# Seven half-width products in place of eight for most FFN column pairs, and a new map of SBUF

## The chip, the core and the metric

The kernel is one program on one core of a Trainium2 chip. The metric is the device time of one execution in microseconds. TensorE (PE) multiplies, VectorE (DVE) and ScalarE (ACT) work on the operands and results, GpSimd (POOL) does a few subtractions at the start and in the mixers, and SyncE (SP) issues the DMAs.

## The reference

Two layers over 512 rows, 256 context tokens and 256 latent tokens, of width 1024. Each layer is a SwiGLU FFN (inner width 2816), a token mixer and a second FFN. Shift, scale and gate of each sub-layer come from `m = silu(c) @ w_ada + b_ada`, nine modulations of 1024 a layer. Cut to what matters:

```
def swiglu(h, w1, w3, w2):
    return (jax.nn.silu(h @ w1) * (h @ w3)) @ w2
...
for l in range(DEPTH):
    x = x + 0.5 * m[:, 2] * swiglu(modulate(rms_norm(x, norm_g[l, 0]), m[:, 0], m[:, 1]), w1[l, 0], w3[l, 0], w2[l, 0])
    ...
    y, yc = token_mixer(h, hc, w_in[l], ...)
    x = x + m[:, 5] * y
    x = x + 0.5 * m[:, 8] * swiglu(modulate(rms_norm(x, norm_g[l, 2]), m[:, 6], m[:, 7]), w1[l, 1], w3[l, 1], w2[l, 1])
```

The context rows xc go through the same FFNs and mixer, up to the last layer's mixer. So three FFNs have 512 tokens, FFN(0,0), FFN(0,1) and FFN(1,0), and the last, FFN(1,1), has 256.

## The kernel before

**Products.** Every big product runs as three matmuls in fp32r (`mm3`, L280 to L282). Weights come as 512 KB loads (8 k-tiles of 128 rows make the 1024 inputs; one load is 4 k-tiles by 256 columns) into `wraw` (pool `wr`, 4 buffers, queue of SP). ACT rounds them to `whi` (L285) and DVE forms `wlo = wraw - whi` (L286), both in pool `wh`, 4 buffers, so a cast waits until the products have read the buffer four chunks earlier. The inputs are kept in the same two parts, `hhi` and `hlo`, as [feature, token].

**An FFN** takes the 2816 columns as 11 pairs g of 256 columns of w1 and 256 of w3, in two halves (g = 0 to 5 and 6 to 10). A pair is 2 x 8 k-tiles x 2 column tiles x 3 = 96 matmuls of 512 tokens ("x512"; x256 is the same for 256). ACT then takes silu of p1 (L607), DVE multiplies by p3 (L608), and ACT and DVE split the result into `ghi` and `glo`. After each half `to_residual` multiplies them by w2 in four column groups `cg`; the last one of the second half is woven with the entry into the next stage (`handover`), where the first pair (g = 0) of the next FFN is computed too.

**Modulations.** `ada` makes one modulation: eight loads of w_ada (512 KB each), two DVE operations of 128x1024 for each (L208 the first, L210 the others), then a few matmuls. `tick()` spreads these steps over the pairs and the w2 groups of the three 512-token FFNs.

**Order.** Apart from the start and the handovers, which are written out by hand, a scheduler sets the order of instructions on each engine when the program is built; each engine and the SP queue then run in that order, and waits between engines are semaphores. A semaphore wait for a tile in PSUM covers the whole two-bank tile.

**SBUF.** From the bottom: constants up to 28 KiB a partition, `xT` to 44, the inputs `hhi` and `hlo` to 76, `wraw` to 92, `whi` and `wlo` to 124, small tiles to 133, and above that the pools of the stages, with `ghi` and `glo`. So the inputs and the weights lie below 128 KiB, and the gated values above. The mixers' inputs are `hhi_m` and `hlo_m` in the same place; their big products are pg and pj (x512 in layer 0, x256 in layer 1).

## Time and profile before

| | us |
|---|---|
| device time, median of 3 runs (2012.78 to 2013.74) | 2013.01 |
| the profiled execution, its own time | 2012.76 |
| its span, first to last instruction | 2011.0 |
| PE busy in the span | 1981.5 (99%) |
| DVE busy | 1330.9 (66%) |
| ACT busy | 836.3 (42%) |

The span lies 1.76 us below the execution's own time. Busy time of matmuls overlaps, since they are pipelined: the mean of one matmul in a group is longer than the step from one start to the next, and what a product costs is read from the steps in the timeline.

### The profile page before, as it was taken

Reading aid. Unit: us, or ns where it says so; the run is one execution under the profiler, and the core shown is the slowest. Engines: PE = TensorE matmul, PEld = TensorE weight load, DVE = VectorE, ACT = ScalarE, POOL = GpSimd, SP = SyncE. Lnnn points to the kernel's source line nnn. Section 1 sums busy time; section 2 is a strip of 40 time slices with the busy share of each in tenths; the row PEclk is TensorE's granted clock in tenths of the full one; section 3 lists DMA queues with packets and bytes.
Section 4 is the critical chain, followed back from the end, with each engine's and each line's share of the span. In section 5 each row is a group of like instructions: output and inputs, shape, how many; then the busy total and the mean of one; then the engine's idle time right before and its main releaser. Section 6 shows DMA issues by size and latency. Waiting matters only on the chain.

```text
span 2011.0 us, 27970 instructions
## 1 busy us (share of the span) xinstructions
PE 1981.5 (99%) x11087; PEld 1685.1 (84%) x11087; DVE 1330.9 (66%) x2038; ACT 836.3 (42%) x1286; POOL 51.7 (3%) x32
## 2 busy tenths in 40 slices
PE   7999999999999999999999999999999998999998
PEld 5887788898777788988788798877888988899998
DVE  6876666476588655765666566664665679877555
ACT  4432222365476534422122243221323758666443
POOL 2000000000001110000000000000000001110000
PEclk8999999999999999999999999999999999999999
DMA  9655555422213324354555425554553224465663
GB/s 298 217 178 173 172 172 173 115 97 83 77 53 97 118 89 123 120 160 146 176 168 157 134 69 189 178 156 125 166 168 105 64 88 143 145 196 162 187 185 115
DMA packets 240507, 288.47 MB, mean 143 GB/s; under 512 B 14368, under 2 KB 222328, under 8 KB 240120
## 3 DMA queue, kind: packets, MB, share of 16 engines
q1 hardware_dynamic: 240376, 286.69, 46.3%
q8 instruction: 87, 1.43, 0.3%
q14 instruction: 44, 0.36, 0.1%
HBM read 283.50 MB, written 3.15 MB: 143 GB/s over the span
## 4 chain that ended last, share of the span: by engine, by line
PE 92%; DVE 3%; ACT 2%; DMA 2%; issue 1%; POOL 0%; SPq 0%; DVEq 0%; ACTq 0%; POOLq 0%
PE p L280 14%; PE p L281 14%; PE p L282 14%; PE py L280 8%; PE py L281 8%; PE py L282 8%; PE pg L282 3%; PE pg L281 3%; PE pg L280 3%; PE pj L281 2%; PE pj L280 2%; PE pj L282 2%; PE pv L809 1%; PE pv L810 1%; PE pv L811 1%; DMA wada<-w_ada 1%
## 5 line engine op out<-in xcount | busy, mean ns | idle before, releaser
L285 ACT CAST whi<-wraw 128x1024 fp32r<-128x1024 f32 (+2 forms) x408 | 406.4, 1000 | 943.6 <-PE p L281 417.0
L286 DVE TENSOR_TENSOR wlo<-wraw,whi 128x1024 fp32r<-128x1024 f32 (+2 forms) x380 | 445.0, 1177 | 348.4 <-ACT whi L285 347.4
L280 PE MATMUL p<-hhi_f,whi 128*128 128x512 f32 (+1 forms) x1440 | 516.1, 359 | 0.4 <-DVE hhi_f L352 0.4
L282 PE MATMUL p<-hhi_f,wlo 128*128 128x512 f32 (+1 forms) x1440 | 513.3, 356 | 1.1 <-POOL wlo L286 0.6
L281 PE MATMUL p<-hlo_f,whi 128*128 128x512 f32 (+1 forms) x1440 | 513.9, 357 | 0.2
L280 PEld LDWEIGHTS p<-hhi_f,whi 128*128 128x128 f32 x1440 | 272.3, 189 | 48.3 <-ACT whi L285 5.9
L282 PEld LDWEIGHTS p<-hhi_f,wlo 128*128 128x128 f32 x1440 | 272.3, 189 | 41.1 <-POOL wlo L286 1.3
L210 DVE SCALAR_TENSOR_TENSOR aacc<-wada,cs,aacc 128x1024 f32<-128x1024 f32 x224 | 277.3, 1279 | 42.6 <-DMA wada<-w_ada 42.3
L281 PEld LDWEIGHTS p<-hlo_f,whi 128*128 128x128 f32 x1440 | 272.3, 189 | 38.8 <-DVE hlo_f L357 1.0
L280 PE MATMUL py<-ghi,whi 128*128 128x512 f32 (+1 forms) x764 | 269.0, 352 | 0.0
L281 PE MATMUL py<-glo,whi 128*128 128x512 f32 (+1 forms) x764 | 267.6, 350 | 0.0
L282 PE MATMUL py<-ghi,wlo 128*128 128x512 f32 (+1 forms) x764 | 267.5, 350 | 0.0
L280 PEld LDWEIGHTS py<-ghi,whi 128*128 128x128 f32 x764 | 143.9, 188 | 26.1 <-issue 4.2
L282 PEld LDWEIGHTS py<-ghi,wlo 128*128 128x128 f32 x764 | 143.9, 188 | 21.3
L281 PEld LDWEIGHTS py<-glo,whi 128*128 128x128 f32 x764 | 143.9, 188 | 21.0
L280 PE MATMUL pg<-hhi_m,whi 128*128 128x512 f32 (+1 forms) x384 | 132.5, 345 | 0.0
L282 PE MATMUL pg<-hhi_m,wlo 128*128 128x512 f32 (+1 forms) x384 | 130.6, 340 | 1.3 <-DVE wlo L286 1.2
L281 PE MATMUL pg<-hlo_m,whi 128*128 128x512 f32 (+1 forms) x384 | 130.3, 339 | 0.0
L286 POOL TENSOR_TENSOR wlo<-wraw,whi 128x768 fp32r<-128x768 f32 (+2 forms) x28 | 51.5, 1842 | 1732.0 <-ACT whi L285 1675.0
L507 DVE SCALAR_TENSOR_TENSOR xT<-py,gmod,xT 128x256 f32<-128x256 f32 x136 | 59.1, 478 | 54.5 <-PE py L282 54.2
L280 PE MATMUL pj<-hhi_m,whi 128*128 128x256 f32 (+1 forms) x288 | 92.9, 323 | 0.0
L281 PE MATMUL pj<-hlo_m,whi 128*128 128x256 f32 (+1 forms) x288 | 92.7, 322 | 0.2
(270 smaller groups left out, 2525.0 us busy)
## 6 DMA issues: line engine op xcount, KB each, us to landing
wraw<-ffn_w SPq DMA_DIRECT2D x256, 512.0 KB, 3.8
wada<-w_ada SPq DMA_DIRECT2D x128, 512.0 KB, 3.8
wraw<-w_in SPq DMA_DIRECT2D x64, 512.0 KB, 3.6
wada<-w_ada SPq DMA_DIRECT2D x32, 256.0 KB, 6.8
wraw<-w_out SPq DMA_DIRECT2D x16, 512.0 KB, 3.4
wraw<-w_in SPq DMA_DIRECT2D x16, 384.0 KB, 3.4
wraw<-w_in SPq DMA_DIRECT2D x20, 256.0 KB, 3.0
wraw<-ffn_w SPq DMA_DIRECT2D x16, 256.0 KB, 2.7
```

Source lines behind the costliest of these rows:

```text
L210: v.scalar_tensor_tensor(acc[:, t], w, cs[:, k, t:t + 1], acc[:, t], op0=ALU.mult, op1=ALU.add)
L280: te.matmul(o, a, xh, start=start, stop=False)
L281: te.matmul(o, a, xl, start=False, stop=False)
L282: te.matmul(o, b, xh, start=False, stop=stop)
L285: s.copy(hi, src)
L286: eng.tensor_tensor(lo, src, hi.bitcast(F32), ALU.subtract)
L507: v.scalar_tensor_tensor(X[0][:, d, c], acc, gate[:, d, t:t + 1], X[0][:, d, c], op0=ALU.mult, op1=ALU.add)
L809: te.matmul(o, hhi[:, kk, ts], hi[:, k], start=(kk == 0), stop=False)
L810: te.matmul(o, hhi[:, kk, ts], lo[:, k], start=False, stop=False)
L811: te.matmul(o, hlo[:, kk, ts], hi[:, k], start=False, stop=(kk == KD - 1))
```

## The change

**Seven products for eight.** For pairs 3 to 10 of the three 512-token FFNs, the two column blocks (w1, w3), the two halves of the 1024 inputs and the two halves of the tokens make a 2 x 2 by 2 x 2 block product. It is computed with seven block products in place of eight (Winograd's form of Strassen): `seven` has seven calls of `part`, each 24 matmuls x256 (4 k-tiles x 2 column tiles x 3). In the code's order they are called P1 to P7 here. P1, P2, P3, P5, P6 and P7 go into one PSUM tile `pab` (b and c are its two halves), P4 into `pc`. A pair is then 168 matmuls x256.

Around them a pair gets four sums of raw weights on DVE (128x1024: L659, L663, L669, L673), seven casts on ACT and seven subtractions on DVE in place of four of each (the weights of the seven products), three copies out of PSUM on ACT (L656, L661, L665), three adds out of PSUM on DVE (L668, L671, L675), and silu and multiply in halves (L678 to L682). The sums of inputs are made once in each FFN by `Forms` (during g = 1 and 2: 8 DVE operations of 128x1024 and four splits).

**Places.** `sm`, `wraw` (now 5 buffers), `whi`/`wlo` and the stage pools with `ghi`/`glo` come first, below 128 KiB; the sums of inputs, `hhi`/`hlo` and `xT` go to the top, above 128 KiB. Two zones there are shared by several short-lived tiles. In FFN(1,1) the gated values lie in those zones.

**Modulations.** The steps of `ada` leave the seven-product pairs: FFN(0,0) makes modulations 2 to 5 of layer 0 (before 2 to 7), mixer 0 gets 6, 7 and 8, FFN(0,1) makes 0 to 3 of layer 1, FFN(1,0) 4 to 7, FFN(1,1) gets 8. In the 512-token FFNs the ticks come at g = 2 and in `to_residual`.

```diff
     const = ctx.enter_context(tc.tile_pool(name="const", bufs=1))
-    xp = ctx.enter_context(tc.tile_pool(name="xp", bufs=1))
-    hp = ctx.enter_context(tc.tile_pool(name="hp", bufs=1))
-    wr = ctx.enter_context(tc.tile_pool(name="wr", bufs=4))
+    sm = ctx.enter_context(tc.tile_pool(name="sm", bufs=2))
+    wr = ctx.enter_context(tc.tile_pool(name="wr", bufs=5))
     wh = ctx.enter_context(tc.tile_pool(name="wh", bufs=4))
-    sm = ctx.enter_context(tc.tile_pool(name="sm", bufs=2))
+    ctx.enter_context(tc.tile_pool(name="pad", bufs=1)).tile([P, 8], F32, name="pad")
+    xp = ctx.enter_context(tc.tile_pool(name="xp", bufs=1, side="right"))
+    hp = ctx.enter_context(tc.tile_pool(name="hp", bufs=1, side="right"))
+    tz = ctx.enter_context(tc.tile_pool(name="tz", bufs=1, side="right"))
+    sp = ctx.enter_context(tc.tile_pool(name="sp", bufs=1, side="right"))
+    hp.tile([P, 16], F32, name="pad")
     ps = ctx.enter_context(tc.tile_pool(name="ps", bufs=2, space=bass.MemoryType.PSUM))
-    ctx.enter_context(tc.tile_pool(name="shift", bufs=1)).tile([P, 8], F32, name="shift")
+    def zone(i, dt=F32):
+        return tz.tile([P, 3 * D], dt, tag=f"t{i}", name=f"zone{i}")
+    def half_zone(i, dt=F32):
+        return sp.tile([P, 3 * NTOK], dt, tag=f"v{i}", name=f"half{i}")
...
-            ws.append(xi.tile([P, 2, 2, L], F32, tag="wada", name="wada", bufs=16))
+            ws.append(last_wada if q == 3 and k == KD - 2 else
+                      xi.tile([P, 2, 2, L], F32, tag="wada", name="wada", bufs=15))
...
+    class Forms:
+        def __init__(self, norm, fp):
+            hi, lo = norm.hi, norm.lo
+            q = [[(x[:, 4 * c:4 * c + 4, 0:L], x[:, 4 * c:4 * c + 4, L:]) for x in (hi, lo)] for c in range(2)]
+            (h11, h12), (l11, l12) = q[0]
+            (h21, h22), (l21, l22) = q[1]
+            z = [zone(i, F32R).rearrange("p (a k n) -> p a k n", a=3, k=4) for i in range(2)]
+            t = [half_zone(i)[:, 0:D].rearrange("p (k n) -> p k n", k=4) for i in range(2)]
+            t.append(fp.tile([P, 2, D], F32, tag="aacc", name="ft")[:, 0].rearrange("p (k n) -> p k n", k=4))
+            def whole(o, a, b):
+                v.tensor_tensor(o, a.bitcast(F32), b.bitcast(F32), ALU.add)
+            whole(t[0], h11, l11)
+            whole(t[1], h12, l12)
+            whole(t[2], h22, l22)
+            v.tensor_tensor(t[0], t[0], t[1], ALU.subtract)
+            v.tensor_tensor(t[1], t[2], t[1], ALU.subtract)
+            split_act(z[0][:, 0], z[1][:, 0], t[0])
+            split_act(z[0][:, 2], z[1][:, 2], t[1])
+            v.scalar_tensor_tensor(t[0], t[0], -1.0, t[2], op0=ALU.mult, op1=ALU.subtract)
+            whole(t[1], h21, l21)
+            split_act(z[0][:, 1], z[1][:, 1], t[0])
+            v.scalar_tensor_tensor(t[0], t[0], -1.0, t[1], op0=ALU.mult, op1=ALU.subtract)
+            self.fourth = lambda: split_act(h12, l12, t[0])
+            self.b11, self.b21, self.b22, self.t4 = (h11, l11), (h21, l21), (h22, l22), (h12, l12)
+            self.t1, self.t2, self.t3 = ((z[0][:, i], z[1][:, i]) for i in range(3))
+            self.n = 0
+        def places(self):
+            if self.n == 0:
+                self.half = [half_zone(i) for i in range(2)]
+                self.w1 = sp.tile([P, NTOK], F32, tag="w1", name="w1")
+            return [x[:, 2 * NTOK:] for x in self.half] + [self.w1]
+        def sum_place(self):
+            self.n += 1
+            return self.half[self.n % 2][:, 0:D].rearrange("p (k n) -> p k n", k=4)
+    def seven(fm, wa, wb, c0, gt):
+        q1, p5, w1 = fm.places()
+        pab, pc = psum("p1"), psum_bg("p3")
+        b, c, a = pab[:, 0], pab[:, 1], pc[:, 0]
+        def raw(w, i):
+            return load_raw([rowsof(w, 4 * i, 4, c0, 2 * P)], 4, 2 * P)
+        def part(o, w, x, first=False):
+            whi, wlo = split(w, 4, 2 * P)
+            for k in range(4):
+                for m in range(2):
+                    om, cm = o[:, m * L:(m + 1) * L], slice(m * P, (m + 1) * P)
+                    for n, (wt, xt) in enumerate(((whi, x[0]), (whi, x[1]), (wlo, x[0]))):
+                        te.matmul(om, wt[:, k, cm], xt[:, k], start=(first and k == m == n == 0),
+                                  stop=(k == 3 and m == 1 and n == 2), skip_group_check=True)
+        a11 = raw(wa, 0)
+        part(b, a11, fm.b11, True)
+        s.copy(q1, b)
+        a21, a22 = raw(wb, 0), raw(wb, 1)
+        s1 = fm.sum_place()
+        v.tensor_tensor(s1, a21, a22, ALU.add)
+        part(c, s1, fm.t1, True)
+        s.copy(p5, c)
+        s2 = fm.sum_place()
+        v.tensor_tensor(s2, s1, a11, ALU.add)
+        part(b, s2, fm.t2)
+        s.copy(w1, b)
+        a12 = raw(wa, 1)
+        part(a, a12, fm.b21, True)
+        v.tensor_tensor(q1, a, q1, ALU.add)
+        v.tensor_tensor(a21, a21, a11, ALU.add)
+        part(b, a21, fm.t3)
+        v.tensor_tensor(p5, b, p5, ALU.add)
+        s4 = fm.sum_place()
+        v.tensor_tensor(s4, s2, a12, ALU.add)
+        part(c, s4, fm.b22)
+        v.tensor_tensor(w1, c, w1, ALU.add)
+        g1, g2 = gt[:, :, 0:L], gt[:, :, L:]
+        q1, p5, w1, b3 = (x.rearrange("p (m n) -> p m n", m=2) for x in (q1, p5, w1, b))
+        s.activation(g1, q1, AF.Silu)
+        s.activation(g2, w1, AF.Silu)
+        v.scalar_tensor_tensor(g2, p5, -1.0, g2, op0=ALU.mult, op1=ALU.mult)
+        part(b, a22, fm.t4)
+        v.scalar_tensor_tensor(g1, b3, -1.0, g1, op0=ALU.mult, op1=ALU.mult)
...
+        both = nt == NTOK
         with tc.tile_pool(name=f"ffn{l}{f}", bufs=1) as fp:
-            steps = (ada(*m, fp) for m in mods)
-            pending[:] = [x for x in steps]
-            total = len(mods) * (KD + 1)
-            state = [0, 0]
-            def tick():
-                state[0] += 1
-                want = min(total, -(-total * state[0] // 56))
+            pending[:] = [ada(*m, fp) for m in mods]
+            due = [0.0]
+            rates = (1.25, (len(mods) * (KD + 1) - 5) / 20) if both else (0.8, 0.0)
+            def tick(rate):
+                due[0] += rate
+                n = int(due[0] + 1e-6)
+                due[0] -= n
                 with norm.done():
-                    background(want - state[1])
-                state[1] = max(want, state[1])
+                    background(n)
+            def weights(n):
+                if both:
+                    return weight_places(n)
+                return [tuple(fp.tile([P, 4, 2 * P], F32R, name=f"e{i}{x}") for x in ("hi", "lo")) for i in range(n)]
             for half, (g0, g1) in enumerate(((0, 6), (6, 11))):
                 nk = 2 * (g1 - g0)
-                ghi = fp.tile([P, 12, NTOK], F32R, tag="ghi", name="ghi")
-                glo = fp.tile([P, 12, NTOK], F32R, tag="glo", name="glo")
+                if both:
+                    ghi = fp.tile([P, 12, NTOK], F32R, tag="ghi", name="ghi")
+                    glo = fp.tile([P, 12, NTOK], F32R, tag="glo", name="glo")
+                else:
+                    ghi, glo = (zone(i, F32R).rearrange("p (k n) -> p k n", k=12) for i in range(2))
                 for g in range(g0, g1):
+                    j = slice(2 * (g - g0), 2 * (g - g0) + 2)
+                    gt = fp.tile([P, 2, NTOK], F32, tag="gt", name="gt")[:, :, 0:nt]
+                    if both and g > 2:
+                        seven(fm, w1, w3, g * 2 * P, gt)
+                        split_act(ghi[:, j, 0:nt], glo[:, j, 0:nt], gt)
+                        continue
                     p1, p3 = norm.accs if g == 0 else (psum("p1"), psum_bg("p3"))
                     if g > 0:
                         for acc, w in ((p1, w1), (p3, w3)):
                             product(acc, load(w, KD, g * 2 * P), (hhi, hlo), nt)
-                            tick()
-                            tick()
-                    j = slice(2 * (g - g0), 2 * (g - g0) + 2)
-                    gt = fp.tile([P, 2, NTOK], F32, tag="gt", name="gt")[:, :, 0:nt]
+                            if g == 2 or not both:
+                                tick(rates[0])
+                                tick(rates[0])
                     if g == 0 and norm.early:
                         norm.gated(gt)
                     else:
                         s.activation(gt, p1[:, :, 0:nt], AF.Silu)
                         v.tensor_tensor(gt, gt, p3[:, :, 0:nt], ALU.mult)
                     split_act(ghi[:, j, 0:nt], glo[:, j, 0:nt], gt)
-                for _ in to_residual(w2, nk, (ghi, glo), nt, gmod[l][:, f], st if half else None, fp, ("a", "b", "c"), 2 * g0,
+                    if both and g == 1:
+                        with norm.done():
+                            fm = Forms(norm, fp)
+                    if both and g == 2:
+                        fm.fourth()
+                for _ in to_residual(w2, nk, (ghi, glo), nt, gmod[l][:, f], st if half else None, fp, weights, 2 * g0,
                                      then):
-                    tick()
+                    tick(rates[1])
+        assert not pending or next(pending[0], None) is None
...
+            pending[:] = [ada(*m, mp) for m in mods]
+            def tick(n=1):
+                with entry.done():
+                    background(n)
...
                         drain()
+                    tick()
...
-                run(merged(2, psum_bg, mm))
-                mhi = mm.tile([P, KD, NTOK], F32R, name="mhi")
-                mlo = mm.tile([P, KD, NTOK], F32R, name="mlo")
+                for n, _ in enumerate(merged(2, psum_bg, mm)):
+                    tick(n % 4 > 0)
+                mhi = mm.tile([P, KD, nq], F32R, name="mhi")
+                mlo = mm.tile([P, KD, nq], F32R, name="mlo")
                 for d in range(0, KD, 2):
                     split_act(mhi[:, d:d + 2, 0:nq], mlo[:, d:d + 2, 0:nq], mixed[d // 4][:, d % 4:d % 4 + 2])
-                run(to_residual(I["w_out"][l], KD, (mhi, mlo), nq, gmod[l][:, 2], st, mm, ("v", "a"), entry=then))
+                for n, _ in enumerate(to_residual(I["w_out"][l], KD, (mhi, mlo), nq, gmod[l][:, 2], st, mm, weight_places,
+                                                  entry=then)):
+                    tick(2)
...
-    ffn(0, 0, NTOK, after, [(0, m) for m in range(2, 8)], entry)
+    ffn(0, 0, NTOK, after, [(0, m) for m in range(2, 6)], entry)
     load_mixer_consts()
     with after.done():
         for l in range(DEPTH):
             mixer_scalars(l)
     after = ffn_entry(0, 1, NTOK)
-    mixer(0, NTOK, entry, after)
+    mixer(0, NTOK, entry, [(0, m) for m in (6, 7, 8)], after)
     load_bias(1)()
     entry = ffn_entry(1, 0, NTOK)
-    ffn(0, 1, NTOK, after, [(0, 8)] + [(1, m) for m in range(4)], entry)
+    ffn(0, 1, NTOK, after, [(1, m) for m in range(4)], entry)
     after = mixer_entry(1)
-    ffn(1, 0, NTOK, entry, [(1, m) for m in range(4, 9)], after)
+    ffn(1, 0, NTOK, entry, [(1, m) for m in range(4, 8)], after)
     entry = ffn_entry(1, 1, L)
-    mixer(1, L, after, entry)
-    ffn(1, 1, L, entry, [], Output())
+    mixer(1, L, after, [], entry)
+    ffn(1, 1, L, entry, [(1, 8)], Output())
...
-    nc = _bacc.Bacc("TRN2", target_bir_lowering=False, num_devices=1)
+    nc = _bacc.Bacc("TRN2", target_bir_lowering=False, num_devices=1, dynamic_dma_scratch_size=1024)
```

**Order on PE at the seam of two pairs**, FFN(0,0) in the kernel before: p_2086 is the p3 of pair g = 8, p_2228 the p1 of g = 9.

```order
L282 MATMUL p_2086<-hhi_f_124,wlo 128x512
L280 MATMUL p_2086<-hhi_f_124,whi 128x512
L281 MATMUL p_2086<-hlo_f_125,whi 128x512
L282 MATMUL p_2086<-hhi_f_124,wlo 128x512
L280 MATMUL p_2228<-hhi_f_124,whi 128x512
L281 MATMUL p_2228<-hlo_f_125,whi 128x512
L282 MATMUL p_2228<-hhi_f_124,wlo 128x512
```

One accumulation follows the other. In the changed kernel, the same FFN, pair g = 8 (p_2503 is its `pab`, p_2504 its `pc`, zone_742 and zone_743 the sums of inputs; L651 is the matmul in `part`):

```order
L651 MATMUL p_2503<-hhi_f_130,wlo 128x256
L651 MATMUL p_2504<-hhi_f_130,whi 128x256
L651 MATMUL p_2504<-hlo_f_131,whi 128x256
L651 MATMUL p_2504<-hhi_f_130,wlo 128x256
L651 MATMUL p_2504<-hhi_f_130,whi 128x256
L651 MATMUL p_2503<-zone_742,whi 128x256
L651 MATMUL p_2503<-zone_743,whi 128x256
L651 MATMUL p_2503<-zone_742,wlo 128x256
```

The first row is the last matmul of P1; four matmuls of P4 stand between it and P2. Over the whole pair PE runs: P7 of the pair before, 8 last matmuls of P1, 4 of P4, P2 (24), 13 of P4, P3 (24), 7 of P4, P5 (24), 8 of the next pair's P1, P6 (24), 8 more of it, P7 (24).

**Order on ACT** over one pair, before (L607 is silu of a pair's p1):

```order
L607 ACTIVATE gt<-p_1932 128x1024
L285 CAST whi<-wraw 128x1024 x3
L285 CAST ghi<-gt 128x1024
L285 CAST whi<-wraw 128x1024 x2
L607 ACTIVATE gt<-p_2085 128x1024
```

and now, from the copy after P1 (L656) to the copy after P3 (L665); half_912 and half_913 hold sums of weights and, later, copies of products:

```order
L306 CAST whi<-wraw 128x1024
L306 CAST ghi<-gt 128x1024
L656 COPY half_912<-p_2503 128x512
L306 CAST whi<-wraw 128x1024
L306 CAST whi<-half_912 128x1024
L661 COPY half_913<-p_2503 128x512
L306 CAST whi<-wraw 128x1024
L665 COPY w_914<-p_2503 128x512
```

The first row casts P4's weights, the fourth P5's; the cast ahead of L661 is that of P6's weights, the one ahead of L665 that of P7's.

**Order on DVE** at pair g = 4 of FFN(0,0) in the changed kernel, where the modulation steps of the coming w2 groups begin (L233 is what L210 was):

```order
L668 TENSOR_TENSOR half_912<-p_1139,half_912 128x512
L307 TENSOR_TENSOR wlo<-wraw,whi 128x1024 x2
L671 TENSOR_TENSOR half_913<-p_1138,half_913 128x512
L307 TENSOR_TENSOR wlo<-half_913,whi 128x1024
L673 TENSOR_TENSOR half_913<-half_912,wraw 128x1024
L233 SCALAR_TENSOR_TENSOR aacc<-wada,cs,aacc 128x1024
L675 TENSOR_TENSOR w_914<-p_1138,w_914 128x512
```

One modulation step stands between the sum L673 and the add L675, for which P7 waits.

## Rows read from the trace of the kernel before

**Rows 1.** the page: span, busy time of engines, shares of the last chain

```profile
span 2011.0 us, 27970 instructions
...
PE 1981.5 (99%) x11087; PEld 1685.1 (84%) x11087; DVE 1330.9 (66%) x2038; ACT 836.3 (42%) x1286; POOL 51.7 (3%) x32
...
PE 92%; DVE 3%; ACT 2%; DMA 2%; issue 1%; POOL 0%; SPq 0%; DVEq 0%; ACTq 0%; POOLq 0%
```

**Rows 2.** windows: us, busy us of each engine, clock, DMA share, GB/s

```profile
55.00:142.00 87.00, 87.00 (x390) 71.15 (x389) 72.41 (x123) 34.02 (x35) 0.00 (x0) 1.00 0.63 194
```

**Rows 3.** timeline (start us, us, engine, operation): x512 matmuls of w1, w3

```profile
99.80 0.39 PE L280 MATMUL p<-hhi_f,whi 128*128 128x512 f32 x1
...
103.20 0.39 PE L280 MATMUL p<-hhi_f,whi 128*128 128x512 f32 x1
```

**Rows 4.** timeline: x512 matmuls of w2 in the same FFN

```profile
200.20 0.39 PE L281 MATMUL py<-glo,whi 128*128 128x512 f32 x1
...
207.20 0.39 PE L281 MATMUL py<-glo,whi 128*128 128x512 f32 x1
```

**Rows 5.** timeline: x256 matmuls of w1 and w3 in the last FFN

```profile
1849.77 0.28 PE L280 MATMUL p<-hhi_f,whi 128*128 128x256 f32 x1
...
1856.49 0.28 PE L282 MATMUL p<-hhi_f,wlo 128*128 128x256 f32 x1
```

**Rows 6.** timeline: x256 matmuls of w2 in the last FFN

```profile
1989.87 0.28 PE L280 MATMUL py<-ghi,whi 128*128 128x256 f32 x1
...
1991.91 0.28 PE L280 MATMUL py<-ghi,whi 128*128 128x256 f32 x1
```

**Rows 7.** groups, shapes apart: count, busy us, mean ns, idle before

```profile
L280 PE MATMUL p<-hhi_f,whi 128*128 128x512 f32 x992 | 389.1, 392 | 0.0
...
L280 PE MATMUL py<-ghi,whi 128*128 128x512 f32 x468 | 185.8, 397 | 0.0
...
L280 PE MATMUL p<-hhi_f,whi 128*128 128x256 f32 x448 | 127.1, 284 | 0.4 <-DVE hhi_f L352 0.4
...
L280 PE MATMUL py<-ghi,whi 128*128 128x256 f32 x296 | 83.2, 281 | 0.0
```

**Rows 8.** the page's part 5: products of the mixers, both shapes together

```profile
L280 PE MATMUL pg<-hhi_m,whi 128*128 128x512 f32 (+1 forms) x384 | 132.5, 345 | 0.0
...
L280 PE MATMUL pj<-hhi_m,whi 128*128 128x256 f32 (+1 forms) x288 | 92.9, 323 | 0.0
```

**Rows 9.** timeline: a sum of DVE that TensorE waits for

```profile
1827.89 1.21 DVE L286 TENSOR_TENSOR wlo<-wraw,whi 128x1024 fp32r<-128x1024 f32 x1
...
1829.16 0.39 PE L282 MATMUL p<-hhi_f,wlo 128*128 128x256 f32 x1 [0.55 <-DVE wlo L286]
...
1829.38 0.28 PE L280 MATMUL p<-hhi_f,whi 128*128 128x256 f32 x1
```

**Rows 10.** timeline: end of an accumulation and the DVE instruction that waits for it

```profile
1987.71 0.28 PE L282 MATMUL py<-ghi,wlo 128*128 128x256 f32 x1
...
1988.03 0.48 DVE L507 SCALAR_TENSOR_TENSOR xT<-py,gmod,xT 128x256 f32<-128x256 f32 x1
```

**Rows 11.** groups of ACT and DVE with shapes apart; the page's w_ada group

```profile
L285 ACT CAST whi<-wraw 128x1024 fp32r<-128x1024 f32 x344 | 359.9, 1051 | 852.9 <-PE p L281 405.4 <-PE py L281 226.1 <-DMA wraw<-ffn_w 111.5
...
L985 ACT COPY aT<-pT 128x512 f32<-128x512 f32 x24 | 14.1, 587 | 12.2 <-PE pT L984 12.1
...
L286 DVE TENSOR_TENSOR wlo<-wraw,whi 128x1024 fp32r<-128x1024 f32 x340 | 413.9, 1221 | 299.8 <-ACT whi L285 298.9
...
L210 DVE SCALAR_TENSOR_TENSOR aacc<-wada,cs,aacc 128x1024 f32<-128x1024 f32 x224 | 277.3, 1279 | 42.6 <-DMA wada<-w_ada 42.3
```

**Rows 12.** timeline: an add of 128x512 out of PSUM

```profile
1838.47 0.68 DVE L608 TENSOR_TENSOR gt<-gt,p 128x512 f32<-128x512 f32 x1
```

**Rows 13.** the page's part 6: DMA issues, KB each, median us to landing

```profile
wraw<-ffn_w SPq DMA_DIRECT2D x256, 512.0 KB, 3.8
...
wada<-w_ada SPq DMA_DIRECT2D x32, 256.0 KB, 6.8
```

## The prediction

> **What bounds the kernel now.** I read the page's busy times and the shares of the chain first: PE is busy 1981.5 of 2011.0 us and holds 92% of the chain [rows 1]. Then the windows: in four pairs of the first FFN PE is busy all of 87.00 us at a granted clock of 1.00, DVE 72.41 and ACT 34.02 [rows 2]. So an FFN costs what its matmuls cost, and DVE has the next largest load. What a matmul costs stands in the timeline as the step from one start to the next. The x512 products of w1 and w3 go from 99.80 to 103.20 in 15 steps: 226.7 ns [rows 3]. Those of w2 take 7.00/30 = 233.3 ns [rows 4]. In the last FFN it is the other way round for x256: 6.72/56 = 120.0 ns for w1 and w3 [rows 5], 2.04/18 = 113.3 ns for w2 [rows 6]. What the two slow or fast ones share is the place of the operands: weights and inputs both below 128 KiB in rows 3 and 5, weights below and gated values above in rows 4 and 6. I read it as: x512 is 6.6 ns shorter with both operands in one half of SBUF, x256 6.7 ns shorter with them in different halves.

> **The seven products.** A pair was 96 x 0.2267 = 21.76 us; 4 x 21.76 = 87.0 is the window of rows 2. It becomes 168 matmuls x256, weights below and inputs above: 168 x 0.1133 = 19.04 (20.16 if the step were that of rows 5). 3 FFNs x 8 pairs x (21.76 - 19.04) = -65.3 us, if PE never waits.

> It will wait, by the order of the changed kernel. The prices of the links: from the start of the last matmul x256 of an accumulation to the DVE instruction that waits for it 1988.03 - 1987.71 = 0.32 us [rows 10]; from the end of a DVE or ACT instruction to the matmul that waits 1829.16 - 1829.10 = 0.06, and the step after such a stop is 0.22 in place of 0.12, so each stop costs 0.1 more [rows 9]. A cast of weights takes 1.05, a copy of 128x512 out of PSUM 0.59, a `wlo` 1.22 [rows 11], a DVE add out of PSUM 0.68 [rows 12]. For the sums of weights the trace of before has no row of its own; they are DVE operations of the same size and operands as `wlo` and I take 1.22 (the range of like rows is 1.22 to 1.28). In a steady pair PE stops at four places:
> - P4's weights lie in the buffer that P7 of the pair before has read, four chunks earlier in a ring of four. The cast can start 0.32 after P7's last-but-one matmul, which is 0.21 after the last; 0.21 + 1.05 + 0.03 + 1.22 + 0.06 = 2.57 us after that start the third matmul of P4, the first with `wlo`, can go. PE has 8 matmuls of P1 and two of P4 in between, and would be there after 11 x 0.113 = 1.25. Wait 1.3, with restarts 1.44. P2 waits for the copy after P1 (L656), which ACT reaches after the cast of P4's weights and that of `ghi`; by the same links it ends at about the same time, so it adds nothing.
> - P3 overwrites P1's place and waits for the copy after P2 (L661), the same tile. On ACT it stands behind the cast of P6's weights, whose buffer P2 has just read: 0.21 + 1.05 + 0.59 + 0.06 = 1.91, less 14 x 0.113 = 1.59 (13 matmuls of P4): 0.31.
> - P5 waits in the same way for L665 behind the cast of P7's weights: 1.91 less 8 x 0.113 = 0.91 (7 matmuls of P4): 1.0.
> - P6 waits for L671 and P7 for L675, each an add out of PSUM: 0.32 + 0.68 + 0.06 = 1.06 less 9 x 0.113 = 1.02: 0.04 and a restart, 0.14 each.

> The sum is 3.03 us, so a steady pair takes 22.07 us against 21.76. The fills differ a little from pair to pair (3 to 8 matmuls of P1): 2.9 to 3.6 in the six steady pairs of an FFN, 19.2 together; the first of each half has better ones, 1.8 (g = 3) and 1.1 (g = 6). 22.1 us an FFN, **+66.3** in all. Bounds: 0 if a fill hides every stop; twice this if DVE is late as well (a rival below). By load neither DVE (some 17 of 22 us) nor ACT (11) bounds a pair.

> **Places elsewhere.** Counts are three times those of the first of three lines. Of 2976 x512 matmuls p [rows 7] 672 stay, now with operands in different halves: 672 x 6.6 ns = +4.4. 1404 py x512: -9.3. 1344 p x256 (the early first pairs and the last FFN): -8.9. Of 888 py x256, the 360 of the last groups whose weights lay above as well: -2.4. Of pg and pj [rows 8], 816 x512 in mixer 0: +5.4, 960 x256 in mixer 1: -6.4; the rest of the mixers -1.7. Sum **-18.9**.

> [...]

> **What comes on top**, each bounded from both sides:
> - Modulation steps in DVE's order ahead of L675 near the end of each half: two of 1.28 us [rows 11] against less than 2 us of slack: 1 us at each of six places, +6 (0 to 15).
> - 16 w_ada operations (20 us of DVE) in mixer 0's token products: +3 (0 to 6). The same number in FFN(1,1), which had none: +2 (0 to 5). Small DVE operations of the mixers' constants that now stand among the first seven-product pairs: +1.5 (0 to 3).
> - Mixer 1's shorter matmuls meet DVE and ACT there, which are not faster: of its 6.4 I give 3 back (0 to 6.4). Mixer 0's longer ones lie partly in such waits: -1.5 (-5.4 to 0).

> Sum **+14** (-5 to +35). Forms (8 sums, 4 splits, about 17 us of DVE and ACT beside 43 us of x512 products), the fifth buffer, and the deleted steps of `ada` in the pairs cost nothing beyond that, PE covers them; if Forms came late, the first seven-product pair would start by so much later.

> **Sum.** 2011.0 - 65.3 + 66.3 - 18.9 + 14 = 2007.1 us of span; the execution of before lay 1.76 above its span and 0.25 below the median: **2009.1 us**, 0.2% below 2013.01. That is near the edge of what a measurement tells from no change (0.2%, about 4 us: below 2009.0 is faster, above 2017.0 slower).

> **Rivals.**
> - *Most waits are covered.* Only P4's stop remains (the ring is a fixed distance), because the other copies and adds come earlier than I chain them: 24 x 1.44 = 34.6 in place of 66.3, about **1977**. For it: three of the four stops are differences of under 1 us. Against: they are chains of durations from rows, and ACT's order sets them.
> - *DVE falls behind the weights, slower.* In DVE's order the first sum of the next pair (L659) stands ahead of the `wlo` of P6, and it needs the load of a21 and a22; the last load is issued once P4's `wlo` is done. With 3.8 us to land [rows 13] I chain the `wlo` of the next P1 to about 0.8 us before PE wants it. So it decides when the load takes more than 4.7 us. At 6.0, near the 6.8 that w_ada loads took where many were in flight [rows 13], each pair loses 1.3: 24 x 1.3 = 31, about **2040**. Against: the DMA share in rows 2 is 0.63, and the pairs now carry no w_ada loads.
> - *The half does not matter.* If rows 3 to 6 differ for another reason (w2 against w1, say), a seven-product pair is 168 x 0.120 = 20.16: -38.4 in place of -65.3, and places give 0 in place of -18.9: about **2055**. [...]

> **Chances.** The forecast 0.50, waits covered 0.20, DVE behind 0.25, no half 0.05. The forecast's own range, from the bounds of the last list and half a microsecond a pair, is 1994 to 2026; about 0.22 of its 0.50 lies below 2009.0, 0.17 within 0.2%, 0.11 above. Faster 0.22 + 0.20 = 0.42, same 0.17 and a little of the others: 0.18, slower 0.40. The range leaves out half of the first rival and, above, "no half" and the worse half of "DVE behind" in part: 1977 to 2042.

> **What would show it.** The step in a seven-product pair is 0.113 and PE stops at P4, P3, P5; the waits of PE name L306 (weights of P4), L661 and L665, with about 3 us a pair; windows of four pairs are 88 us. L671 or `wlo` as longer waits mean the second rival, a step of 0.120 the third. w2 products at 0.227, mixer 1 shorter by 3 us, mixer 0 longer by 5 to 8 show the other terms. I am wrong if the pair takes under 21 or over 23 us.

## Result and the profile after

The changed kernel takes **2079.24 us** (median of 4 runs, 2077.63 to 2079.86) against 2013.1 before: a ratio of 1.0327 (95% interval 1.0309 to 1.0345), 3.3% slower. The forecast of 2009 us and its range are both missed. PE holds 78% of the chain where it held 92% [rows 1]; DVE, idle gaps of issue, ACT and DMA took the rest. The page after (span, busy time and instructions of each engine, shares of the last chain):

```profile
span 2077.7 us, 31966 instructions
...
PE 1988.9 (96%) x12815; PEld 1743.1 (84%) x12815; DVE 1617.2 (78%) x2338; ACT 957.5 (46%) x1466; POOL 53.8 (3%) x32
...
PE 78%; DVE 9%; issue 5%; ACT 4%; DMA 4%; POOL 0%; SPq 0%; DVEq 0%; ACTq 0%; POOLq 0%
```

DVE has 286 us more to do [rows 1]. The list of PE's waits (waiting operation, what ended the wait, us in total, times, longest us) names the places where PE stood:

```profile
PE py L303 <- DVE wlo L307: 14.5, 7, 3.1
PE p L651 <- DVE wlo L307: 14.3, 21, 0.8
PE p L651 <- ACT w L665: 10.8, 13, 2.1
PE p L651 <- ACT whi L306: 8.1, 13, 1.0
PE p L303 <- DVE wlo L307: 4.7, 2, 4.3
PE p L651 <- DVE w L675: 2.9, 5, 1.2
```

L651, the seven products, waits for the weights (L306 and L307) and for the copy L665, as forecast; the copy L661 ended waits of 0.6 us in all. For 13.6 of the 14.3 us spent on `wlo`, DVE began that `wlo` 0.03 us after ACT had ended the cast (as at 290.10 below): the cast came late, not DVE. The two lines with L303 are in products by eight: w2, mixer 0's output and FFN(1,1).

**Where the 66.7 us of span went**, by the starts of each stage's first matmul in the traces (us; FFN(0,0) is counted from the same matmul of its first pair in both, behind the waits of the start; FFN(1,1) includes the end of the kernel):

```
              start  FFN(0,0)  mixer 0  FFN(0,1)  FFN(1,0)  mixer 1  FFN(1,1)
before         45.8     362.2    402.7     374.4     373.8    254.1     198.0
after          46.5     374.4    418.6     390.1     386.2    254.5     207.3
difference     +0.7     +12.2    +15.9     +15.7     +12.4     +0.4      +9.3
```

**One pair.** In a steady pair the stop at P5 comes back after 300.95 - 278.17 = 22.78 us. Timeline of the changed kernel (start us, us, engine, line, operation, idle before and what ended it), the stop at P5 twice and the chains to the two largest stops:

```profile
278.17 0.50 PE L651 MATMUL p<-zone,whi 128*128 128x256 f32 x2 [0.72 <-ACT w L665]
...
289.02 1.05 ACT L306 CAST whi<-wraw 128x1024 fp32r<-128x1024 f32 x1 [2.29 <-issue]
...
290.10 1.22 DVE L307 TENSOR_TENSOR wlo<-wraw,whi 128x1024 fp32r<-128x1024 f32 x1 [0.32 <-ACT whi L306]
...
291.38 0.39 PE L651 MATMUL p<-hhi_f,wlo 128*128 128x256 f32 x1 [0.76 <-DVE wlo L307]
...
299.37 1.05 ACT L306 CAST whi<-wraw 128x1024 fp32r<-128x1024 f32 x1 [3.10 <-issue]
...
300.32 0.58 ACT L665 COPY w<-p 128x512 f32<-128x512 f32 x1
...
300.95 0.39 PE L651 MATMUL p<-zone,whi 128*128 128x256 f32 x1 [0.72 <-ACT w L665]
```

The cast of P4's weights ends at 290.07, `wlo` follows, and P4's third matmul goes 0.06 after it: the chain of the forecast. The cast of P7's weights stands ahead of L665 on ACT, and P5 goes when L665 is done. The stops are as forecast; the step is not:

```profile
282.29 0.28 PE L651 MATMUL p<-hlo_f,whi 128*128 128x256 f32 x1
...
284.77 0.28 PE L651 MATMUL p<-hlo_f,whi 128*128 128x256 f32 x1
```

21 steps, 118.1 ns, neither the 113.3 of [rows 6] nor the 120.0 of [rows 5]. And w2, whose operands are now both below 128 KiB:

```profile
199.78 0.39 PE L301 MATMUL py<-ghi,whi 128*128 128x512 f32 x1
...
207.01 0.40 PE L302 MATMUL py<-glo,whi 128*128 128x512 f32 x1
```

31 steps, 233.2 ns, as in [rows 4] and not the 226.7 of [rows 3]. So this pair is 168 x 0.1182 = 19.86 us of products and 2.92 us of stops, 22.78, where eight products took 21.76: the seven products cost 1.0 us a pair. By place, restarts included, the stops are 1.4 us at P4, 0.3 at P3, 1.0 at P5 and 0.1 each at P6 and P7. In all 24 pairs what goes beyond a step adds up to about 71 us.

### The profile page after: what moved, and what is told of

Same layout as the page of the kernel before. It is cut to its first block, busy times and chain, and to the rows that moved or that the text cites. A ratio compares the mean times of both kernels' runs of the same rounds, so it can differ in the third digit from the quotient of the medians.

```text
span 2077.7 us, 31966 instructions
## 1 busy us (share of the span) xinstructions
PE 1988.9 (96%) x12815; PEld 1743.1 (84%) x12815; DVE 1617.2 (78%) x2338; ACT 957.5 (46%) x1466; POOL 53.8 (3%) x32
## 4 chain that ended last, share of the span: by engine, by line
PE 78%; DVE 9%; issue 5%; ACT 4%; DMA 4%; POOL 0%; SPq 0%; DVEq 0%; ACTq 0%; POOLq 0%
PE p L651 17%; PE py L301 8%; PE py L303 8%; PE py L302 7%; PE p L302 4%; PE p L303 4%; PE p L301 4%; DVE wlo L307 3%; PE pg L303 3%; PE pg L302 3%; PE pg L301 3%; DMA wada<-w_ada 2%; ACT whi L306 2%; PE pj L302 2%; PE pj L301 2%
## 5 line engine op out<-in xcount | busy, mean ns | idle before, releaser
L306 ACT CAST whi<-wraw 128x1024 fp32r<-128x1024 f32 (+2 forms) x392 | 391.4, 1002 | 620.8 <-issue 158.3
L307 DVE TENSOR_TENSOR wlo<-wraw,whi 128x1024 fp32r<-128x1024 f32 (+2 forms) x364 | 426.6, 1181 | 151.7 <-ACT whi L306 146.1
L233 DVE SCALAR_TENSOR_TENSOR aacc<-wada,cs,aacc 128x1024 f32<-128x1024 f32 x224 | 279.3, 1294 | 9.3 <-DMA wada<-w_ada 9.0
L651 PE MATMUL p<-hhi_f,whi 128*128 128x256 f32 x768 | 220.4, 289 | 12.0 <-ACT whi L306 8.1
L651 PE MATMUL p<-hhi_f,wlo 128*128 128x256 f32 x768 | 214.8, 284 | 14.4 <-DVE wlo L307 14.3
L651 PE MATMUL p<-zone,whi 128*128 128x256 f32 x1152 | 214.1, 286 | 13.2 <-ACT w L665 10.8
L303 PE MATMUL p<-hhi_f,wlo 128*128 128x256 f32 (+1 forms) x672 | 216.1, 322 | 5.3 <-DVE wlo L307 4.7
L301 PE MATMUL p<-hhi_f,whi 128*128 128x256 f32 (+1 forms) x672 | 216.9, 323 | 0.4 <-DVE hhi_f L373 0.4
L302 PE MATMUL p<-hlo_f,whi 128*128 128x256 f32 (+1 forms) x672 | 216.1, 322 | 0.3
L651 PE MATMUL p<-hlo_f,whi 128*128 128x256 f32 x768 | 215.1, 281 | 0.0
L651 PEld LDWEIGHTS p<-zone,whi 128*128 128x128 f32 x1152 | 177.4, 190 | 27.1 <-ACT w L665 18.8
L303 PE MATMUL py<-ghi,wlo 128*128 128x512 f32 x468 | 185.5, 396 | 11.5 <-DVE wlo L307 11.5
L301 PE MATMUL py<-ghi,whi 128*128 128x512 f32 x468 | 186.9, 399 | 0.0
L302 PE MATMUL py<-glo,whi 128*128 128x512 f32 x468 | 185.2, 396 | 0.0
L651 PEld LDWEIGHTS p<-hhi_f,whi 128*128 128x128 f32 x768 | 144.5, 188 | 22.3 <-ACT whi L306 13.0
L651 PE MATMUL p<-zone,wlo 128*128 128x256 f32 x576 | 162.3, 282 | 0.0
L651 PEld LDWEIGHTS p<-hhi_f,wlo 128*128 128x128 f32 x768 | 143.5, 188 | 18.9 <-DVE wlo L307 18.9
L306 ACT CAST whi<-half 128x1024 fp32r<-128x1024 f32 x72 | 75.6, 1050 | 169.3 <-PE p L651 134.0
L651 PEld LDWEIGHTS p<-hlo_f,whi 128*128 128x128 f32 x768 | 144.7, 188 | 0.3
L303 PEld LDWEIGHTS p<-hhi_f,wlo 128*128 128x128 f32 x672 | 127.6, 190 | 16.6 <-DVE wlo L307 5.2
```

The costliest lines, as they stand in the source:

```text
L233: v.scalar_tensor_tensor(acc[:, t], w, cs[:, k, t:t + 1], acc[:, t], op0=ALU.mult, op1=ALU.add)
L301: te.matmul(o, a, xh, start=start, stop=False)
L302: te.matmul(o, a, xl, start=False, stop=False)
L303: te.matmul(o, b, xh, start=False, stop=stop)
L306: s.copy(hi, src)
L307: eng.tensor_tensor(lo, src, hi.bitcast(F32), ALU.subtract)
```

## Experiments

### What sets the step: the half of SBUF, or the offset of the two operands

My reading of rows 3 to 6 was that the 128 KiB halves count. The addresses in the program allow another: in the kernel before, inputs and weights of w1 and w3 both start 96 bytes above a multiple of 512, ghi 288 bytes. In the changed kernel the weights start at 256, ghi at 288, the inputs at 480 and the zones at 416. Half and offset change together between rows 3 and 4. Two runs of the kernel before separate them, each with only an unused tile at the bottom of each FFN's pool:

```diff
         with tc.tile_pool(name=f"ffn{l}{f}", bufs=1) as fp:
+            fp.tile([P, {(0, 0): 80, (0, 1): 16, (1, 0): 112, (1, 1): 80}[l, f]], F32, name="pad")
```

> The kernel before, with an unused tile at the bottom of each FFN's pool, so that ghi and glo (and the weights of the last column group) move up by some bytes and nothing else changes. The start of ghi less the start of the weights, modulo 512 bytes, is 192 in the kernel before; here it is 0 in FFN(0,0), 256 in FFN(0,1), 128 in FFN(1,0) and 0 in FFN(1,1). Theory 'half' (the prediction's: what counts is whether the two operands lie in the same 128 KiB half): the w2 products keep their steps, 233.3 ns x512 in the three 512-token FFNs and 113.3 ns x256 in FFN(1,1), span 2011. Theory 'offset' (what counts is how the two starts stand to each other within some 512 bytes or less): FFN(0,0) falls to 226.7 ns (468 x512 matmuls x 6.6 ns = -3.1 us), FFN(1,1) rises to 120.0 ns (about 480 x256, +3.2 us), and FFN(0,1) and FFN(1,0) show what 256 and 128 do: 226.7 in FFN(0,1) if only the offset within 256 or less counts.

Measured: 2009.9 us (one run; the kernel before beside it 2012.89), span 2008.1. The w2 products of FFN(0,0) and then of FFN(1,1) in b_pads1:

```profile
199.25 0.39 PE L280 MATMUL py<-ghi,whi 128*128 128x512 f32 x1
...
206.50 0.39 PE L282 MATMUL py<-ghi,wlo 128*128 128x512 f32 x1
```

```profile
1987.81 0.28 PE L280 MATMUL py<-ghi,whi 128*128 128x256 f32 x1
...
1991.89 0.28 PE L281 MATMUL py<-glo,whi 128*128 128x256 f32 x1
```

32 steps of 226.6 ns and 34 of 120.0, though the operands lie in different halves as before. The half plays no part in it: 226.7 is also the step of [rows 3], where both lie in one half at the same offset 0. The second kernel has pads of 88, 96, 120 and 88 elements in the same order.

> The same edit with other sizes: ghi less weights, modulo 512, is 32 in FFN(0,0), 64 in FFN(0,1), 160 in FFN(1,0) and 32 in FFN(1,1). Theory 'half': 233.3 ns x512 everywhere and 113.3 ns x256 in FFN(1,1). Theory 'offset': the step depends on the number; in the changed kernel, with 32, 160 and 224, x512 took 233.3 and x256 116 to 118.3 ns, so FFN(1,1) goes from 113.3 to about 118 ns (+2.4 us) and FFN(0,0) and FFN(1,0) stay at 233.3.

Measured: 2013.38 us (one run). Its w2 in FFN(0,0), at offset 32 in different halves, steps at 233.3 ns, as does the w2 of the changed kernel, at offset 32 in one half. The steps of all these runs, as means over neighbouring matmuls of one size (start of the moving operand less start of the stationary one, modulo 256 bytes):

```
offset    x512 ns         x256 ns            seen in
  0       226.9 to 227.5  119.8 to 120.0     before, b_pads1 (0 and 256), a_offsets
 32       233.3           116.7 to 117.8     after, b_pads2
 64       229.0           117.8, once 113.4  b_pads2 (x512), a_offsets (x256)
128       233.3           118.7 to 119.5     b_pads1, after
160       234.0 to 234.3  118.1              b_pads2, after
192       233.3           113.3 or 117.8     before, a_offsets
224       233.3           118.3              after
```

FFN(0,1) of b_pads1, at 256, takes the 226.9 ns of offset 0, so the table counts modulo 256. The changed kernel sits at 32, 160 and 224, where neither size is at its shortest. a_offsets mends that by 32 and 64 bytes:

```diff
-    wr = ctx.enter_context(tc.tile_pool(name="wr", bufs=5))
-    wh = ctx.enter_context(tc.tile_pool(name="wh", bufs=4))
-
     ctx.enter_context(tc.tile_pool(name="pad", bufs=1)).tile([P, 8], F32, name="pad")
+    wr = ctx.enter_context(tc.tile_pool(name="wr", bufs=5))
+    wh = ctx.enter_context(tc.tile_pool(name="wh", bufs=4))
...
-    hp.tile([P, 16], F32, name="pad")
```

> The changed kernel, with its two pads placed otherwise: raw weights and weights start 32 bytes higher, the zones above 128 KiB 64 bytes higher; no tile changes its half, no instruction its place. Inputs and zones less weights, modulo 512, become 192 (before the edit 224 and 160), ghi less weights 0 (32). Theory 'half': the steps stay 118.3 ns x256 and 233.3 ns x512, 2079 us. Theory 'offset': the seven-product pairs step at 113.3 ns, 24 x 168 x 4.9 ns = -19.8 us; the other x256 products of w1, w3 and mixer 1 about -11; the w2 products x512 at 226.7 ns, 1404 x 6.6 ns = -9.3; together about -40, 2039 us, less what the shorter pairs give back in waits.

Measured: **2055.61 us**, ratio to the kernel before 1.0214 (1.0197 to 1.0232), 23.6 us less than the changed kernel, and w2 at 227.5 ns. The sign is that of the offset theory, the size falls short of 40: the mean step x256 at offset 192 is 114.6, not 113.3, and the stops inside the pairs grew (the six stretches of seven products take 557.8 us in place of 563.9, although their matmuls alone should save about 14). A shorter product covers less of a chain of fixed length.

### Do the seven products gain or lose

a_eight is the changed kernel with eight products in all pairs and no sums of inputs:

```diff
-                    if both and g > 2:
+                    if False:
...
-                    if both and g == 1:
-                        with norm.done():
-                            fm = Forms(norm, fp)
-                    if both and g == 2:
-                        fm.fourth()
```

> The changed kernel with all eleven pairs by eight products and without the sums of inputs; places, modulation steps and everything else as in the changed kernel. If the seven products cost time, as the trace of the changed kernel says (a steady pair 22.78 us against 96 x 0.2333 = 22.40 by eight at this place), it is some 10 to 25 us faster than the changed kernel, 2054 to 2069. If the loss lies in places and modulation steps alone and the seven products save time, as they would with all waits covered (19.9 us a pair), it is slower than the changed kernel: 24 x 2.5 = 60 us, 2140. If the predicted sum of waits and savings (+1 us) held, it is within 5 us of 2079.

Measured: 2066.84 us (1.0268, 1.0253 to 1.0284), 12.4 us faster than the changed kernel. So the seven products, with their stops, cost 12 us at that place: half a microsecond a pair, and the first of the three cases. The other 54 us against the kernel before are there without any seven products.

### What makes the stops

If P1 to P7 wait because b and c share a PSUM tile, one line should help:

```diff
-        b, c, a = pab[:, 0], pab[:, 1], pc[:, 0]
+        b, a, c = pab[:, 0], pc[:, 0], pc[:, 1]
```

In the changed kernel P2 must wait for the copy of P1's result although it writes the other half of the tile (that copy, L656, ended waits of PE of 1.3 us in all), and P3 for that of P2 (L661, 0.6 us); the scheduler then fills with pieces of P4, whose weights are the last to come. With the edit neighbours in the order lie in different tiles, and PE's order becomes P1 to P7, 24 matmuls each.

> The changed kernel with one line edited: of the three results of a pair, b keeps the first half of pab, and c moves from pab's other half into pc, beside a (b, a, c = pab[:, 0], pc[:, 0], pc[:, 1]). No product, sum or copy changes. Each product then goes into another PSUM tile than the one before it, so it does not wait for the copy or add that reads its forerunner, and the order on PE becomes P1, P2, P3, P4, P5, P6, P7, 24 matmuls each. Theory 'tile' (the stops of a pair come from b and c sharing one tile, which sets the waits and with them the order): 24 matmuls of another tile, 2.8 us, cover each chain of 1.1 to 2.6 us, the stops vanish, a pair goes from 22.8 us to 168 x 0.1182 = 19.9, and the kernel to 2079 - 24 x 2.9 = about 2009 us. Theory 'load' (ACT and DVE, in their order, cannot feed seven splits a pair faster): DVE has 17 to 18 us of work a pair and hops between engines besides; the pair stays above 21.5 us and the kernel above 2050.

Measured: 2009.23 us, ratio 0.9978 (0.9968 to 0.9987): 70.0 us less, where 24 x 2.9 = 70 was expected. The same group of matmuls with `wlo`, before and after the edit (line, operation, count, busy us, mean ns, idle before and what ended it), in the changed kernel and in a_banks:

```profile
L651 PE MATMUL p<-hhi_f,wlo 128*128 128x256 f32 x768 | 214.8, 284 | 14.4 <-DVE wlo L307 14.3
```

```profile
L651 PE MATMUL p<-hhi_f,wlo 128*128 128x256 f32 x768 | 215.8, 281 | 0.0
```

14.3 us of waiting are gone from this group, and PE's busy time in 96 us of the last five pairs of FFN(1,0) (window, PE busy, PEld, DVE, ACT, POOL, clock, DMA share, GB/s; the changed kernel, then a_banks) rises from 92% to nearly all:

```profile
1440.00:1536.00 96.00, 88.46 (x706) 84.61 (x705) 78.97 (x77) 44.24 (x54) 0.00 (x0) 1.00 0.35 105
```

```profile
1384.00:1480.00 96.00, 95.57 (x810) 95.36 (x809) 88.61 (x88) 52.53 (x63) 0.00 (x0) 1.00 0.41 127
```

DVE does 88.6 us of work in 96 there, so the theory 'load' falls: DVE can feed the pairs, with about 8% to spare. The same line in a_offsets:

> The same line edited in a_offsets (weights and inputs with the offsets that make x256 shortest). Theory 'tile': a pair becomes 168 x 0.1135 = 19.1 us where it is 22.0 now, 24 x 2.9 = -70 from 2055.6, about 1986 us, below the kernel before. Theory 'load': DVE's 17 to 18 us a pair leave about 1 us; the pair stays at 21 us or more and the kernel at 2030 or more. Between them: about 20 us a pair, 2007, if DVE binds in some pairs.

Measured: 1987.77 us, ratio **0.9875** (0.9858 to 0.9891). Less by 67.8 us than a_offsets.

### What the modulation steps cost

> a_offsets with the modulations' DVE work cut: of each modulation's 16 DVE operations of 128x1024 (8 loads, 2 each) only 4 are done, those of the first two loads; all loads and matmuls stay. What is left out is the rest of the sum over the inputs, so the modulations are other numbers. If the waits for wlo in the w2 products, in mixer 0's output product and in FFN(1,1) (13.1 + 4.8 us in a_offsets) come from these operations standing ahead of it in DVE's order, they go, and the mixers shorten a little: 2030 to 2038 us. The stops inside the seven-product pairs, 40 us in that kernel's list of waits, stay as they are, within 5 us. If DVE's load in whole were what slows the pairs, these would shorten too, by more than 10 us.

```diff
-                else:
+                elif k == 1:
                     v.scalar_tensor_tensor(acc[:, t], w, cs[:, k, t:t + 1], acc[:, t], op0=ALU.mult, op1=ALU.add)
```

Measured: 2014.3 us (one run), 41 us less than a_offsets, more than the 18 to 26 expected. The waits of PE for `wlo` in the w2 products and mixer 0's output are gone from its list; in FFN(1,1) 2.6 us are left:

```profile
PE p L650 <- ACT w L664: 12.5, 19, 1.4
PE p L650 <- DVE wlo L306: 9.1, 12, 0.8
PE p L650 <- ACT whi L305: 8.4, 18, 1.0
...
PE p L302 <- DVE wlo L306: 2.6, 2, 2.0
```

My expectation for the pairs was wrong: their stops of over 0.25 us fell from 60 to 45 us in all, not by under 5, since steps of w_ada also stood in DVE's order in pairs 3 to 5. The expectation had set a fall of more than 10 us down to DVE's load in whole. Against that stands a_banks, where DVE has all of this work and is busier (88.6 of 96 us) but the stops are nearly gone; three quarters of the stops stayed here. So DVE's modulation work is a cause of its own, and part of it sits inside the pairs. (The six stretches of seven products are only 2.3 us shorter than in a_offsets, since 12 us of other matmuls, of the modulations and w2, moved into them.)

e_offsets asks what the moved steps cost without any seven products: a_eight, with pads that bring the offsets back to what they were before.

```diff
+    xp.tile([P, 48], F32, name="pad")
...
+    hp.tile([P, 16], F32, name="pad")
...
-                    if both and g > 2:
+                    if False:
```

(the other lines as in a_offsets and a_eight.)

> All eleven pairs by eight products as in a_eight, but with pads that give every product the offset it had in the kernel before: inputs and gated values less weights 0 (modulo 512), FFN(1,1)'s gated values less weights 192 modulo 256, weights and values above and below 128 KiB as in the changed kernel. The steps become those of the kernel before (226.7 and 120.0 ns) or better in w2 (226.7), so what is left against the kernel before is what the moved modulation steps and the shared zones cost. Theory 'offset': 2066.8 - 6.6 ns x (about 2800 x512 of w1, w3 and the mixer + 1404 of w2) = -28, and +1.7 ns x 3000 x256 = +5: about 2044. Theory 'half': no step changes against a_eight, 2067. If it lands at 2044, the moved steps cost about 31 us against the kernel before, plus the 3 us that w2 gains.

Measured: 2035.46 us (1.0110, 1.0095 to 1.0125); 31.4 us less than a_eight from offsets alone, 9 more than I expected. Against the kernel before its span is 20.8 us longer: +13.1 in mixer 0, +8.1 in FFN(1,1), within 1.3 in each other stage (in the three long FFNs the shorter w2 steps hide about 3 us each). The modulation steps are not free in mixer 0 and FFN(1,1): PE waits up to 3.2 us in products by eight of x512 and 4.2 us in FFN(1,1), both for a `wlo` behind a row of w_ada operations, and the modulations' own matmuls take 4.1 us in mixer 0 and 2.6 in FFN(1,1). The DVE of FFN(1,1) in the changed kernel shows it:

```profile
1893.06 4.87 DVE L233 SCALAR_TENSOR_TENSOR aacc<-wada,cs,aacc 128x1024 f32<-128x1024 f32 x4
...
1897.84 0.68 DVE L734 TENSOR_TENSOR gt<-gt,p 128x512 f32<-128x512 f32 x1
1898.44 1.22 DVE L307 TENSOR_TENSOR wlo<-wraw,whi 128x1024 fp32r<-128x1024 f32 x1
```

The weights were cast by 1895.24; `wlo` started at 1898.44.

Such a stop cost more than itself in places. In mixer 0's output product of the changed kernel PE stands for 2.99 us, and the granted clock behind it is 0.50 before it is 1.00 again; x512 steps at 0.43 us meanwhile, in place of 0.233 (timeline, then windows):

```profile
801.55 0.80 PE L303 MATMUL py<-mhi,wlo 128*128 128x512 f32 x1 [2.99 <-DVE wlo L307]
802.14 0.63 PE L301 MATMUL py<-mhi,whi 128*128 128x512 f32 x1
802.57 0.63 PE L302 MATMUL py<-mlo,whi 128*128 128x512 f32 x1
```

```profile
801.55:804.65 3.10, 3.10 (x7) 2.48 (x8) 3.10 (x4) 1.05 (x1) 0.00 (x0) 0.50 0.54 170
805.00:808.00 3.00, 3.00 (x14) 2.43 (x13) 3.00 (x4) 1.47 (x2) 0.00 (x0) 1.00 0.54 185
```

The kernel before has no stretch at 0.50 between 28 and 2007 us. The changed kernel has four (from 801, 1730 and 1900 us, after stops of 2.99, 1.88 and 4.25 us, and from 1146 us, after stops of 1.22, 0.71 and 0.76 within 6 us), which by their steps cost about 6 us; its stops of 2.14 us at 117 and of 3.09 at 390, 1199 and 1585 us have none behind them. e_offsets has five, about 8 us. In o_few_ada, without most of DVE's modulation work, two are left, about 3 us.

### A version that beats both

o_rates is o_banks with three more modulation steps in pair g = 2:

```diff
-            rates = (1.25, (len(mods) * (KD + 1) - 5) / 20) if both else (0.8, 0.0)
+            rates = (2.0, (len(mods) * (KD + 1) - 8) / 20) if both else (0.8, 0.0)
```

> o_banks with the modulation steps of each 512-token FFN spread otherwise: 8 of them in pair g = 2 (5 before the edit), so 1.4 in each w2 step instead of 1.55. If the waits for wlo in w2 (12.4 us in o_banks) come from too many steps' DVE work in the second half's w2, three steps less (3 x 2.5 us of DVE an FFN) take most of it away: 1978 to 1982 us. If pair g = 2, with the sums of inputs on DVE, cannot take three more, the waits move there and it stays at 1986 to 1990.

Measured: **1969.6 us**, ratio 0.9780 (0.9765 to 0.9794), 18 us less than o_banks, more than the best case. The waits for `wlo` in w2 and mixer 0's output are 6.0 us (12.4), and no stop over 0.2 us is left in the 24 pairs; in o_banks there were 11 of over 0.25, 9.5 us together. The stretches at a granted clock of 0.50 went from five to two, about 6 us more. Some 5 us went the other way, because more of the streams of seven products took the longer of two steps (last section). o_both also moves mixer 0's inputs by 64 bytes within their tile:

```diff
+            o = 16 if self.name == "m0" else 0
+            self.hi, self.lo = (hp.tile([P, KD * NTOK + 64], F32R, tag=x, name=f"{x}_{self.name}")[:, o:o + KD * NTOK]
+                                .rearrange("p (k n) -> p k n", k=KD) for x in ("hhi", "hlo"))
```

> o_rates, and in mixer 0 alone the inputs start 64 bytes higher in their tile, so that they stand 256 bytes from the weights' offset, where x512 took 226.9 ns in b_pads1, in place of 192 (233.3). Theory 'offset': 816 matmuls x512 x 6.5 ns = 5.3 us less than o_rates, some of it given back in that mixer's waits, 3 to 5 us. Theory 'half': the same time as o_rates.

Measured: 1969.12 us (0.9786, 0.9770 to 0.9803): the same as o_rates within the spread. In the profiled executions mixer 0 is 2.1 us shorter (415.0 against 417.1) with x512 at 228 ns; FFN(0,0) is 2.7 longer and FFN(0,1) 3.5 shorter, mostly by which of two steps their streams got (last section). Inconclusive as a gain.

## Why the prediction was wrong

- **What bounds the kernel.** Right: PE's stream of steps sets an FFN's time, 19.86 of the 22.78 us of a steady pair.
- **The seven products' step**, 113.3 ns by "weights below, inputs above": **this is the step that failed**, the reading of rows 3 to 6 that the half of SBUF sets the step. They do differ by 6.6 ns, but with the offset of the operands within 256 bytes: in b_pads1, at offset 0, w2 took 226.6 ns in place of 233.3. The step measured 118.1 to 118.3: 24 x 168 x 4.9 ns = +20 us.
- **Places elsewhere, -18.9:** the same error. w2 stayed at 233 where 226.7 was counted, x256 came to 118 where 113.3 was, while the longer x512 of w1, w3 and mixer 0 came as counted. By the measured steps and the same counts this term is about +8, so +27 against the forecast. Mixer 1 came out 0.4 us longer, not 3 shorter.
- **The stops, +66.3:** right, in its parts too. 1.44, 0.31, 1.0, 0.14 and 0.14 us were chained for P4, P3, P5, P6 and P7, 3.03 in all, and 1.4, 0.3, 1.0, 0.1 and 0.1 measured, 2.92. (The sum leaves out the restart of 0.1 at P3 and at P5 that its own price asks for.) The 24 pairs have about 71 us of stops, against 66.3 and the +6 for modulation steps in them, and taking the shared tile away gave 70 us back. What I did not see is that the stops were no property of the method: one line removed them.
- **What comes on top, +14:** undersized. 70.6 us lie between the forecast span of 2007.1 and the measured 2077.7; 20 + 27 of them are the steps, about 24 are left for this term, so it was near 38. e_offsets supports that: 20.8 us in spite of a faster w2 (-9.3), so about 30 without any seven products. The forecast had +3 for mixer 0 and +2 for FFN(1,1), which took 13 and 8 there. It had no price for waits behind w_ada operations in the second half's w2 and in mixer 0's output product (14.5 us in the list of the changed kernel), nor for the granted clock of 0.50 after stops (about 6 us).
- **The rivals.** "The half does not matter", given 0.05, was the true one in kind: x512 takes 226.7 ns in one half and 226.6 in two at offset 0, 233.2 and 233.3 at offset 32. It supposed 120.0 ns for every x256 and got 2055. "Waits covered" describes a_banks, not this kernel. "DVE behind the weights" did not happen through the load: PE's list has no stop that a weight load ended inside the pairs. The waits for `wlo`, which were to be its sign, did come (14.3 us), but as the chain of P4, with DVE ready.

## What to carry to other kernels

A difference between two rows has as many causes as things that differ between them: list them, addresses included, before one is used to price a new layout; an unused tile of some bytes is a cheap way to part them. In a chain of products that accumulate in PSUM, put neighbours in the order into different tiles: in the changed kernel the wait for a tile covered both its halves (P2 for L656, 1.3 us) and the scheduler built its order around it, and one line against that was worth 70 us of 2079. Background work moved out of one stage needs a stage with room on its engine; look at the window where it will land, and reckon with a slower clock behind a stop of PE: behind two of the changed kernel's six stops of 2 us or more after the start (2.99 and 4.25 us) the granted clock was 0.50.

## What the hardware showed that I had not expected

At offset 192 there were two steps, 113.3 and 117.8 ns (at 64 117.8 and, once, 113.4), and a stream kept the one it had until PE stopped: in the five runs with that offset in the pairs none changed without a stop. In o_rates, FFN(0,0), the stream changes at the only stop inside its pairs (264.21 to 264.40, 0.19 us):

```profile
262.68 0.28 PE L650 MATMUL p<-zone,wlo 128*128 128x256 f32 x1
...
264.09 0.28 PE L650 MATMUL p<-zone,wlo 128*128 128x256 f32 x1
264.21 0.36 PE L650 MATMUL p<-hhi_f,whi 128*128 128x256 f32 x1
264.40 0.28 PE L650 MATMUL p<-hlo_f,whi 128*128 128x256 f32 x1
...
265.10 0.28 PE L650 MATMUL p<-hlo_f,whi 128*128 128x256 f32 x1
...
266.23 0.28 PE L650 MATMUL p<-hhi_f,wlo 128*128 128x256 f32 x1
```

Ahead of it 12 steps take 1.41 us (117.5 ns each), behind it 10 take 1.13 (113 ns). Four of that kernel's six stretches of seven products run at 117.8 from end to end. What decides which step a stream gets was not tried and stays open, and so does why the offset matters.
